# A two-layer trunk with a seven-product input projection: x read transposed, its norm applied to the results, one product of three column groups formed ahead

## The chip, the cores and the metric

The kernel runs on one core of one Trainium2 chip. The metric is the device time of one execution in microseconds (us); the time before is the median of three runs, 1564.92 us (1564.27 to 1565.75). A smaller number is better.

## The reference

Two decoder layers work on 512 tokens of width 2048, all in float32. Layer 0 is gated linear attention (GLA) with 4 heads, layer 1 latent attention (MLA) with 16 heads. Each layer normalizes its input, projects it with one wide matrix, mixes the tokens, multiplies by a SiLU gate, projects back, normalizes again and adds the residual:

```python
h = rms_norm(x, g_pre)
# layer 0
q, k, v, gate, gk_low = split(h @ w_in)        # widths 1024, 1024, 2048, 2048, 16
log_a = log_sigmoid(gk_low @ w_gk2 + b_gk) / 16
b = cumsum(log_a)                              # the decays, within chunks of tokens
o = causal(q*exp(b) @ (k*exp(-b)).T) @ v + (state carried from earlier chunks)
y = (rms_norm(o, g_onorm) * silu(gate)) @ w_out
x = x + rms_norm(y, g_post)
```

rms_norm multiplies each token's row by one number, 1/sqrt(mean of squares), and each column by a gain.

## The kernel before, in words

**Numbers of full width from fast products.** A float32 operand is kept as a rounded part hi (type fp32r) and a rest lo. One product is three matmuls of TensorE (PE): hi by hi, lo by hi, hi by lo (`mm3`, L128 to L132). ScalarE (ACT) rounds hi, VectorE (DVE) subtracts to get lo. Weights arrive as raw tiles through the DMA queue of SyncE (SP) and are split this way on the fly; some small transfers are issued by GpSimd (POOL).

**Seven products.** The projection of layer 0 is a 2x2 block product by the Strassen-Winograd scheme, which needs seven block products instead of eight. Tokens are halved (256 and 256), so are the rows of the weights (even and odd blocks of 128), and a column pair of 2 x 512 columns makes one group. There are six groups: q and k of heads 0 and 1, v and gate of head 0, of head 1, q and k of heads 2 and 3, v and gate of head 2, of head 3. `first_four` (L253) forms four of the seven products for all six groups: 8 pairs of weight rows a group, and for each pair a left and a right tile of 512 KB, three sums on DVE (L262 to L264), hi and lo of four weight blocks (L267 to L270) and 24 matmuls of 128x512. Its results are combined (u, vw) and parked in HBM (`stage`). `last_three` (L286) then takes the groups again, with 18 matmuls a pair, reads the parked results back (`done`) and combines them into c, which an evacuation function of the group takes further.

**The left side.** `start` (L320) reads x by rows, sums its squares on ACT, multiplies by the norm and the gain on DVE, transposes on PE (`xn_t`) and keeps the result h, transposed, in `ht` and, split, in the four slots of `act_hi` and `act_lo`. `left_sums` (L362) makes the sums of h that the first four products need, `left_rest` (L374) those of the last three, after all first products, since they take the same slots. `gk_low` (L499) makes the 16 columns of the decay gate by 16 plain float32 matmuls (`gkl_acc`).

**Around the groups.** `decays` (L535) makes the decays of two heads: matmuls `z`, exponentials on ACT, scans of 512 elements on DVE. `qk_evac` (L579) transposes c on PE (`qk_t`) and multiplies it by the decays. `scores` and `values` are the attention of one head. `values` writes y of a head to HBM, and `gla_rows` (L674) reads all four back, transposes them (`y_t`) and fills `act_hi` and `act_lo` for `out_proj`. That one makes four column blocks of 512, the last as two of 256. MLA follows; its first projection (`cq`) is done as two blocks of 256 columns.

**What sets the order.** The program is written in the order above, and a scheduler orders each engine's instructions at build time by its own estimate; on the chip each engine works its list strictly in order and waits by semaphores. Tiles come from pools with a fixed number of buffers. The pools of the second half of the projection (`wb`, `psb`) are opened where those of the first (`wa`, `psa`) were closed, so that a new tile waits for the old tile that lay in the same place.

Of the kernel before, what the change touches and what calls it, by code (L numbers as in the profile page):

```python
# [14 lines left out]
F32 = DT.float32  # L15
FR = DT.float32r
# [29 lines left out]
NMAC = 6  # L46
GQ0, GK0, GV0, GG0, GL0 = 0, 1024, 2048, 4096, 6144
# [3 lines left out]
R_BGK, R_GON, R_GQA, R_GKV, R_PRE = 0, 8, 12, 16, 20  # L51
NROWS = 36
# [23 lines left out]
class Trunk:  # L76
# [121 lines left out]
    def build(self):  # L198
        tc, a = self.tc, self.a
        from contextlib import ExitStack  # L200
        with ExitStack() as ctx:
# [18 lines left out]
            self.gla_rows()  # L220
# [18 lines left out]
    def raw_pair(self, w, c0, kp, rows=2, name="raw"):  # L239

        t = self.wp.tile([P, rows, 512], F32, tag=f"{name}{rows}", name=name, bufs=3)
        src = w[(2 * kp + 2 - rows) * P:(2 * kp + 2) * P, c0:c0 + 512]
        self.nc.sync.dma_start(t, src.rearrange("(k p) n -> p k n", p=P))
        return t

    def prods(self, ps, kp, slots, hi, lo, ws):
        for q, (slot, wi) in enumerate(zip(slots, ws)):
            for r in range(2):
                self.mm3(ps[2 * q + r], self.act_slot(self.act_hi, kp, slot, r),
                         self.act_slot(self.act_lo, kp, slot, r), hi[:, wi, :], lo[:, wi, :],  # L250
                         kp == 0, kp == KT // 2 - 1)

    def first_four(self, w, m, n1, n2):  # L253


        nc, v = self.nc, self.nc.vector
        ps = [self.ps.tile([P, 512], F32, tag="a", name=f"pa{q}", bufs=8) for q in range(8)]
        for kp in range(KT // 2):
            r1 = self.raw_pair(w, n1, kp, name="left")
            r2 = self.raw_pair(w, n2, kp, name="right")  # L260
            t = self.wp.tile([P, 3, 512], F32, tag="sums", name="sums", bufs=2)
            v.tensor_tensor(t[:, 0, :], r1[:, 0, :], r2[:, 0, :], ALU.add)  # L262
            v.tensor_tensor(t[:, 1, :], t[:, 0, :], r2[:, 1, :], ALU.add)
            v.tensor_tensor(t[:, 2, :], t[:, 1, :], r1[:, 1, :], ALU.add)  # L264
            hi = self.wp.tile([P, 4, 512], FR, tag="w_hi", name="w_hi", bufs=2)
            lo = self.wp.tile([P, 4, 512], FR, tag="w_lo", name="w_lo", bufs=2)
            nc.scalar.copy(hi[:, 0, :], r1[:, 0, :])  # L267
            v.tensor_tensor(lo[:, 0, :], r1[:, 0, :], hi[:, 0, :].bitcast(F32), ALU.subtract)
            nc.scalar.copy(hi[:, 1:4, :], t)  # L269
            v.tensor_tensor(lo[:, 1:4, :], t, hi[:, 1:4, :].bitcast(F32), ALU.subtract)  # L270
            self.prods(ps, kp, (0, 2, 1, 3), hi, lo, (0, 2, 1, 3))
        for r in range(2):
            p1 = self.stg([P, 512], "p1")
            nc.scalar.copy(p1, ps[r])  # L274
            nc.gpsimd.dma_start(self.stage[m, :, 0, r, :], p1)
            u = self.stg([P, 512], "u2")
            v.tensor_tensor(u, p1, ps[2 + r], ALU.subtract)
            for i, p in ((1, ps[4 + r]), (2, ps[6 + r])):
                t = self.stg([P, 512], "vw")
                v.tensor_tensor(t, u, p, ALU.add)  # L280
                nc.gpsimd.dma_start(self.stage[m, :, i, r, :], t)

# [3 lines left out]
    def last_three(self, w, m, n1, n2, evac):  # L286
# [4 lines left out]
        done = self.sp.tile([P, 3, 2, 512], F32, tag="done", name="done", bufs=1)  # L291
        nc.gpsimd.dma_start(done, self.stage[m])
        for kp in range(KT // 2):
            r1 = self.raw_pair(w, n1, kp, 1, name="left")
            r2 = self.raw_pair(w, n2, kp, name="right")
            t = self.wp.tile([P, 512], F32, tag="sum", name="sum", bufs=2)
            v.tensor_tensor(t, r2[:, 0, :], r2[:, 1, :], ALU.add)
            hi = self.wp.tile([P, 3, 512], FR, tag="w_hi", name="w_hi", bufs=2)
            lo = self.wp.tile([P, 3, 512], FR, tag="w_lo", name="w_lo", bufs=2)
            for i, x in enumerate((r1[:, 0, :], r2[:, 1, :], t)):  # L300
                nc.scalar.copy(hi[:, i, :], x)
                v.tensor_tensor(lo[:, i, :], x, hi[:, i, :].bitcast(F32), ALU.subtract)  # L302
            self.prods(ps, kp, (2, 0, 1), hi, lo, (0, 1, 2))
        for r in range(2):
            p2, q3, p7 = ps[r], ps[2 + r], ps[4 + r]
            c = [self.stg([P, 512], f"c{i}") for i in range(4)]
            v.tensor_tensor(c[0], p2, done[:, 0, r, :], ALU.add)
            evac(r, 0, c[0])
            v.tensor_tensor(c[1], q3, done[:, 1, r, :], ALU.subtract)
            evac(r, 1, c[1])  # L310
            v.tensor_tensor(c[2], p7, done[:, 2, r, :], ALU.add)
            evac(2 + r, 0, c[2])
            v.scalar_tensor_tensor(c[3], p7, -1.0, done[:, 1, r, :], ALU.mult, ALU.subtract)
            evac(2 + r, 1, c[3])
# [5 lines left out]
    def start(self):  # L320

# [8 lines left out]
        with tc.tile_pool(name="start", bufs=1, reuse_waits="tile") as xp:  # L330
# [11 lines left out]
            for s in range(ST):  # L342
                parts = self.st.tile([P, 4], F32, tag="parts", name="parts", bufs=2)
                for g in range(4):
                    self.sumsq(xt[s][:, g * 512:(g + 1) * 512], parts[:, g:g + 1])
# [714 lines left out]
```

## Time and profile before

| | us |
|---|---|
| median of three runs | 1564.92 |
| the profiled execution | 1565.73 |
| its span, first to last instruction | 1564.0 |
| PE busy in it | 1463.3 (94%) |
| DVE busy in it | 978.1 (63%) |
| ACT busy in it | 729.7 (47%) |

The profiled execution took 1.7 us more than its span and 0.8 us more than the median. PE is busy nearly everywhere, so the time is PE's list plus what PE waits, plus what it loses where its granted clock (PEclk) is below 1.00. In the tables of stages, a column gives an engine's busy time in the stage and behind it, as x, the number of its instructions; behind the engines stand the mean granted clock, the busy share of the DMA engines and their GB/s. In a timeline a row's second number is how long its instructions took from first to last.

### The profile page before, as it was taken

To read this page: it belongs to the slowest core of one execution; us is meant where nothing else is said; L and a number is where in the kernel's file an instruction comes from. 1 tells how busy PE (TensorE), PEld (TensorE's weight loads), DVE (VectorE), ACT (ScalarE), POOL (GpSimd) and SP (SyncE) were. 2 spreads that over 40 slices of the span, in tenths; PEclk is the share of its full clock that TensorE was granted. 3 is DMA by queue.
4 is the path that set the end of the run, shared out by engine and by line. 5 is a ranking of instruction groups with operands and counts; after the bars stand their busy time and mean duration, and the time that the engine had idled before them with its cause. 6 is when DMAs were issued, how large, how long until landed. Compare 5 with 4: busy or idle time off the path is not lost.

```text
span 1564.0 us, 19919 instructions
## 1 busy us (share of the span) xinstructions
PE 1463.3 (94%) x7409; PEld 1234.4 (79%) x7409; DVE 978.1 (63%) x1652; ACT 729.7 (47%) x1391; POOL 68.6 (4%) x130
## 2 busy tenths in 40 slices
PE   2699999978699799699999999999999999999998
PEld 2287887857588678588899988888888889888888
DVE  6488888879888878544347434344367777863324
ACT  6233343335366446534336424444466666753221
POOL 0200000001000000200001100000000000000000
PEclk7799999999899989799999999999999999999999
DMA  7167777745366555744326223333322221235222
GB/s 283 29 181 223 229 226 226 223 166 188 121 199 192 167 168 163 256 132 126 111 88 227 71 81 105 98 95 94 82 72 70 60 60 51 69 124 171 94 95 108
DMA packets 132961, 216.09 MB, mean 138 GB/s; under 512 B 19628, under 2 KB 56720, under 8 KB 130048
## 3 DMA queue, kind: packets, MB, share of 16 engines
q1 hardware_dynamic: 124064, 178.81, 37.4%
q0 software_dynamic: 8512, 34.89, 6.5%
q8 instruction: 58, 0.95, 0.3%
q10 hardware_dynamic: 288, 1.11, 0.2%
q14 instruction: 39, 0.32, 0.1%
HBM read 192.53 MB, written 22.25 MB: 137 GB/s over the span
## 4 chain that ended last, share of the span: by engine, by line
PE 70%; issue 18%; DVE 6%; DMA 3%; ACT 2%; POOL 1%; SPq 0%; DVEq 0%; POOLq 0%; ACTq 0%
PE yo_acc L130 8%; PE yo_acc L132 8%; PE yo_acc L131 8%; PE pb L130 4%; PE pb L131 4%; PE pb L132 3%; PE acc L132 3%; PE acc L131 3%; PE acc L130 3%; PE q_acc L132 1%; PE q_acc L131 1%; PE q_acc L130 1%; PE pt L1012 1%; DMA right<-in_l_gla_w_in_dram 1%; PE cq_acc L131 1%
## 5 line engine op out<-in xcount | busy, mean ns | idle before, releaser
L131 PE MATMUL yo_acc<-w_hi,act_lo 128*128 128x512 f32 (+1 forms) x440 | 154.1, 351 | 0.0
L132 PE MATMUL yo_acc<-w_lo,act_hi 128*128 128x512 f32 (+1 forms) x440 | 153.0, 349 | 0.0
L130 PE MATMUL yo_acc<-w_hi,act_hi 128*128 128x512 f32 (+1 forms) x440 | 152.8, 349 | 0.0
L130 PE MATMUL pa<-w_hi,act_hi 128*128 128x512 f32 x384 | 150.4, 392 | 1.4 <-ACT p L274 1.4
L131 PE MATMUL pa<-w_hi,act_lo 128*128 128x512 f32 x384 | 149.5, 389 | 0.0
L124 DVE SCALAR_TENSOR_TENSOR w_lo<-w_raw,gcol,w_hi 128x512 fp32r<-128x512 f32 (+1 forms) x98 | 64.6, 698 | 106.6 <-ACT w_hi L123 106.5
L130 PE MATMUL pb<-w_hi,act_hi 128*128 128x512 f32 x288 | 116.4, 408 | 12.7 <-ACT act_hi L384 7.6
L132 PE MATMUL pa<-w_lo,act_hi 128*128 128x512 f32 x384 | 118.3, 389 | 0.0
L123 ACT ACTIVATE w_hi<-w_raw,gcol 128x512 fp32r<-128x512 f32 (+1 forms) x98 | 61.5, 676 | 114.0 <-PE acc L132 83.9
L131 PE MATMUL pb<-w_hi,act_lo 128*128 128x512 f32 x288 | 114.0, 397 | 0.0
L132 PE MATMUL pb<-w_lo,act_hi 128*128 128x512 f32 x288 | 101.0, 398 | 0.8 <-DVE w_lo L302 0.8
L130 PE MATMUL acc<-act_hi,w_hi 128*128 128x512 f32 x256 | 99.7, 389 | 0.0
L131 PE MATMUL acc<-act_hi,w_lo 128*128 128x512 f32 x256 | 99.6, 389 | 0.0
L132 PE MATMUL acc<-act_lo,w_hi 128*128 128x512 f32 x256 | 99.1, 389 | 0.0
L270 DVE TENSOR_TENSOR w_lo<-sums,w_hi 128x1536 fp32r<-128x1536 f32 x48 | 84.2, 1754 | 15.1 <-ACT w_hi L269 15.1
L130 PEld LDWEIGHTS yo_acc<-w_hi,act_hi 128*128 128x128 f32 x440 | 83.7, 190 | 10.5 <-ACT act_hi L179 0.2
L131 PEld LDWEIGHTS yo_acc<-w_hi,act_lo 128*128 128x128 f32 x440 | 83.7, 190 | 10.0
L132 PEld LDWEIGHTS yo_acc<-w_lo,act_hi 128*128 128x128 f32 x440 | 83.6, 190 | 10.0
L116 DVE TENSOR_TENSOR w_lo<-w_raw,w_hi 128x1024 fp32r<-128x1024 f32 x32 | 39.2, 1224 | 80.9 <-ACT w_hi L115 80.8
L130 PEld LDWEIGHTS pa<-w_hi,act_hi 128*128 128x128 f32 x384 | 72.0, 188 | 20.5 <-ACT p L274 3.2
L124 DVE SCALAR_TENSOR_TENSOR w_lo<-w_raw,gon,w_hi 128x512 fp32r<-128x512 f32 (+1 forms) x80 | 47.7, 641 | 59.6 <-ACT w_hi L123 59.3
L132 PEld LDWEIGHTS pa<-w_lo,act_hi 128*128 128x128 f32 x384 | 72.1, 188 | 15.0
(331 smaller groups left out, 3636.9 us busy)
## 6 DMA issues: line engine op xcount, KB each, us to landing
right<-in_l_gla_w_in_dram SPq DMA_DIRECT2D x96, 512.0 KB, 4.3
left<-in_l_gla_w_in_dram SPq DMA_DIRECT2D x48, 512.0 KB, 4.7
w_raw<-in_l_mla_w_in_dram SPq DMA_DIRECT2D x47, 512.0 KB, 3.7
w_raw<-in_l_gla_w_out_dram SPq DMA_DIRECT2D x32, 512.0 KB, 4.0
w_raw<-in_l_mla_w_out_dram SPq DMA_DIRECT2D x32, 512.0 KB, 3.6
left<-in_l_gla_w_in_dram SPq DMA_DIRECT2D x48, 256.0 KB, 3.6
done<-stage POOLq DMA_DIRECT2D x6, 1536.0 KB, 7.4
pw_raw<-in_l_mla_w_kvb_dram SPq DMA_DIRECT2D x64, 128.0 KB, 2.6
```

The source lines that it names most:

```text
L116: nc.vector.tensor_tensor(lo, raw, hi.bitcast(F32), ALU.subtract)
L123: nc.scalar.activation(hi[:, kk, :], raw[:, kk, :], AF.Copy, scale=g)
L124: nc.vector.scalar_tensor_tensor(lo[:, kk, :], raw[:, kk, :], g, hi[:, kk, :].bitcast(F32), ALU.mult, ALU.subtract)
L130: t.matmul(out, lh, rh, start=start, stop=False)
L131: t.matmul(out, ll, rh, start=False, stop=False)
L132: t.matmul(out, lh, rl, start=False, stop=stop)
L270: v.tensor_tensor(lo[:, 1:4, :], t, hi[:, 1:4, :].bitcast(F32), ALU.subtract)
L1012: te.transpose(pt[:, o:o + P], probs[i][:, j * P:(j + 1) * P], self.ident)
```

## The change

- **x comes transposed.** Besides x by rows, the kernel gets x transposed (`xt`) and all gains as columns (`gains`), laid out before the launch. `start` loads rows of `xt` straight into `ht`. Only the gain is multiplied in. The norm is a number per token, so it commutes with the projection: `x_norm` reads x by rows through POOL in 16 tiles of 256 KB, sums the squares on ACT and keeps 1/sqrt in `rcol`, and the evacuations multiply by it (`c<-c,rcol`, `v_hi`, `gate`); the decay gate gets it through a small product (`gkl_r`).
- **One product early.** `first_one` forms the first of the seven products for groups 1 to 3 while the rest of x is still being prepared; it needs only the even rows and the first half of the tokens. `first_four` then has three products left for these groups (18 matmuls a pair of weight rows) and four for groups 4 to 6.
- **Sums in place.** The weight sums are written over the raw tiles; hi and lo of two blocks are made by one instruction each. The sums of the left side are written over `ht` (`left_swap`) well ahead, and `left_rest` only splits them, between the pairs of group 6.
- **Decays ahead.** `decays(0)` stands behind group 2 of the first products. `decays(1)` stands right behind the scores of heads 0 and 1, which are now both made before the first of the two v and gate groups.
- **Reading back.** `last_three` reads the parked results in six tiles of 256 KB with four buffers, each when it is due, instead of one tile of 1.5 MB. y of heads 0 to 2 is read back and transposed inside the last group, y of head 3 never leaves the chip (`y_rows`).
- **Full widths.** The last block of `out_proj` and the first of MLA are now 512 columns wide, over two halves of the rows.

On PE, at the start of the program, before (`xn_t` are transposes of x, `gkl_acc` the decay gate, `pa` the products of group 1):

```order
L353 MATMUL xn_t<-cf,x_89 128x128 x16
L353 MATMUL xn_t<-cf,x_97 128x128 x16
L353 MATMUL xn_t<-cf,x_99 128x128 x16
L353 MATMUL xn_t<-cf,x_101 128x128 x16
L411 MATMUL gcols<-cf,rows 128x36
L504 MATMUL gkl_acc<-ht,gkl_raw 16x512 x16
L130 MATMUL pa_388<-w_hi,act_hi 128x512
```

and of the change, from its sixteenth instruction (`p_0_89`, `p_1_90`: the first product of group 1, `p_0_192` that of group 2):

```order
L132 MATMUL p_1_90<-w_hi,act_lo 128x512
L589 MATMUL gkl_acc<-ht,gkl_raw 16x512
L133 MATMUL p_0_89<-w_lo,act_hi 128x512
...
L133 MATMUL p_1_90<-w_lo,act_hi 128x512
L589 MATMUL gkl_acc<-ht,gkl_raw 16x512 x15
L131 MATMUL p_0_89<-w_hi,act_hi 128x512
...
L131 MATMUL p_0_192<-w_hi,act_hi 128x512
```

The transposes are gone, products stand first, and 15 of the 16 gate matmuls, which read all of `ht`, stand ahead of the last quarter of the first early product.

On DVE, the decays of heads 0 and 1 before (`c` are results of the first group of the last products, `eq` and `ek` the decays, `qk_t` the transposed q and k):

```order
L307 TENSOR_TENSOR c_2815<-pb_2520,done 128x512
L309 TENSOR_TENSOR c_2816<-pb_2522,done 128x512
L554 TENSOR_TENSOR ek<-eq,ek 128x2048
L556 SCALAR_TENSOR_TENSOR eq<-restart,ek 128x512 x4
L563 TENSOR_TENSOR rest<-eq 128x12
L573 TENSOR_TENSOR ek<-eq 128x2048
...
L588 SCALAR_TENSOR_TENSOR eq<-qk_t,eq 128x4x128 x2
```

and of the change, in group 2 of the first products:

```order
L642 TENSOR_TENSOR ek<-eq,ek 128x2048
L302 TENSOR_TENSOR w_lo<-left,w_hi 128x512
L294 TENSOR_TENSOR right<-left,right 128x512
L297 TENSOR_TENSOR left<-right,left 128x512
L253 TENSOR_TENSOR w_lo<-right,w_hi 128x1024
L644 SCALAR_TENSOR_TENSOR eq<-restart,ek 128x512 x4
L295 TENSOR_TENSOR right<-right 128x512
L302 TENSOR_TENSOR w_lo<-left,w_hi 128x512
...
L661 TENSOR_TENSOR ek<-eq 128x2048
```

The same instructions have moved from the end of a group, where `qk_t` needs them, to between the weight splits of an earlier group.

On DVE, at the change from the first to the last products, of the change (`raw` is a weight tile of the last products, `ht` the sums of the left side):

```order
L253 TENSOR_TENSOR w_lo<-left,w_hi 128x1024
L315 TENSOR_TENSOR u_2483<-p_2477,pa_2159 128x512
L315 TENSOR_TENSOR u_2485<-p_2480,pa_2160 128x512
L319 TENSOR_TENSOR vw<-u_2483,pa_2161 128x512
L319 TENSOR_TENSOR vw<-u_2485,pa_2162 128x512
L464 TENSOR_TENSOR act_lo<-ht,act_hi 128x2x768
L319 TENSOR_TENSOR vw<-u_2483,pa_2163 128x512
L319 TENSOR_TENSOR vw<-u_2485,pa_2164 128x512
L349 TENSOR_TENSOR raw<-raw 128x512 x2
L253 TENSOR_TENSOR w_lo<-raw,w_hi 128x1536 x2
```

Before, twenty sums and splits of `left_rest` stood there, with the first weight splits of the last products among them. Now one split of the left side is left, and the first sums of weights stand behind all results of group 6. The first `raw` tile lies where `ht` lay, so its load is issued after that last split of `ht`.

The diff, cut to its core:

```diff
+    def split_w(self, t):
+        hi = self.wp.tile(shape, FR, tag="w_hi", name="w_hi", bufs=self.w_bufs)
+        lo = self.wp.tile(shape, FR, tag="w_lo", name="w_lo", bufs=self.w_bufs)
+        nc.scalar.copy(hi, t)
+        nc.vector.tensor_tensor(lo, t, hi.bitcast(F32), ALU.subtract)
+    def prod(self, ps, kp, slot, wt, i):
+        for r in range(2):
+            self.mm3(ps[r], self.act_slot(self.act_hi, kp, slot, r),
...
+    def first_one(self, w, n1, rows=None):
+        ps = [self.bank("a", f"p1_{r}") for r in range(2)]
...
+            wt = self.split_w(t)
+            for i in range(2):
+                self.prod(ps, 2 * g + i, 0, wt, i)
+        return ps
...
+            v.tensor_tensor(right[:, 0, :], left[:, 0, :], right[:, 0, :], ALU.add)
+            v.tensor_tensor(right[:, 1, :], right[:, 0, :], right[:, 1, :], ALU.add)
+            wr = self.split_w(right)
+            v.tensor_tensor(left[:, 1, :], right[:, 1, :], left[:, 1, :], ALU.add)
+            if have:
...
+            self.prod(ps[0:2], kp, 2, wr, 1)
+            self.prod(ps[2:4], kp, 1, wr, 0)
+            self.prod(ps[4:6], kp, 3, wl, 1)
...
-        done = self.sp.tile([P, 3, 2, 512], F32, tag="done", name="done", bufs=1)
-        nc.gpsimd.dma_start(done, self.stage[m])
...
+        def done(i, r):
+            t = self.sp.tile([P, 512], F32, tag="done", name="done", bufs=4)
+            nc.gpsimd.dma_start(t, self.stage[m, :, i, r, :])
...
+    def x_norm(self):
...
+                t = self.tmp([P, 512], F32, "x")
+                nc.gpsimd.dma_start(t, self.a["x"][0, s * P:(s + 1) * P, g * 512:(g + 1) * 512])
+                self.sumsq(t, parts[:, s, g:g + 1])
...
+    def left_swap(self, g):
+        v.tensor_tensor(h(0, 1), h(0, 0), h(0, 1), ALU.subtract)
+        v.tensor_tensor(h(0, 0), h(1, 0), h(1, 1), ALU.subtract)
+        v.tensor_tensor(h(0, 0), h(0, 0), h(0, 1), ALU.subtract)
...
+                        self.first_four(w, m, n1, n2, early[m] if m < len(early) else None)
+                        if m == 0:
+                            self.x_norm()
+                            self.constants()
+                        if m == 1:
+                            self.gk_low()
+                            self.gk_spread()
+                            with tc.issue_after(self.ln_exp.ins):
+                                self.decays(0)
...
+                    at = [self.scores(h) for h in (2 * p, 2 * p + 1)]
+                    if p == 0:
+                        self.decays(1)
+                    for i, h in enumerate((2 * p, 2 * p + 1)):
+                        self.last_three(w, 3 * p + 1 + i, *vg(h), self.vg_begin(h))
+                        if h == GH - 1:
+                            for e in range(h):
+                                self.y_rows(e)
+                        self.values(h, at[i])
+                self.y_rows(GH - 1)
...
-        self.block_s(w, 1536, 256, 0, ps, hi, lo, KT, gain=gain, evac=evac(3, 1536, 256, 0))
-        self.block_s(w, 1792, 256, 256, ps, hi, lo, KT, gain=gain, evac=evac(4, 1792, 256, 256), resident=True)
+        self.block_s(w, 1536, 512, 0, ps, hi, lo, KT, gain=gain, ks=(0, KT // 2))
+        self.block_s(w, 1536, 512, 0, ps, hi, lo, KT, gain=gain, evac=evac(3, 1536, 512, 0), resident=True,
+                     ks=(KT // 2, KT))
```

More of the change, by code (lines that the diff above doesn't have):

```diff
@@ L244, in raw_pair @@
         return t
-    def prods(self, ps, kp, slots, hi, lo, ws):
-        for q, (slot, wi) in enumerate(zip(slots, ws)):
-            for r in range(2):
[L249 to L271, printed above, removed]
-        for r in range(2):
[L273 to L281, printed above, removed]
@@ new lines, in first_four @@
+    def first_four(self, w, m, n1, n2, p1=None):
+        nc, v = self.nc, self.nc.vector
+        have = p1 is not None
+        ps1 = None if have else [self.bank("t", f"p1_{r}") for r in range(2)]
+        ps = [self.bank("a", f"pa{q}") for q in range(6)]
+        for kp in range(KT // 2):
+            left = self.raw_pair(w, n1, kp, "left")
+            right = self.raw_pair(w, n2, kp, "right")
+            v.tensor_tensor(right[:, 0, :], left[:, 0, :], right[:, 0, :], ALU.add)
[3 more added lines that the diff above has]
+            if have:
+                hi = self.wp.tile([P, 2, 512], FR, tag="w_hi", name="w_hi", bufs=self.w_bufs)
+                lo = self.wp.tile([P, 2, 512], FR, tag="w_lo", name="w_lo", bufs=self.w_bufs)
+                nc.scalar.copy(hi[:, 1, :], left[:, 1, :])
+                v.tensor_tensor(lo[:, 1, :], left[:, 1, :], hi[:, 1, :].bitcast(F32), ALU.subtract)
+                wl = hi, lo
+            else:
+                wl = self.split_w(left)
+                self.prod(ps1, kp, 0, wl, 0)
+            self.prod(ps[0:2], kp, 2, wr, 1)
+            self.prod(ps[2:4], kp, 1, wr, 0)
+            self.prod(ps[4:6], kp, 3, wl, 1)
+        if not have:
+            p1 = self.p1_out(m, ps1)
+        u = []
+        for r in range(2):
+            u.append(self.stg([P, 512], "u2"))
+            v.tensor_tensor(u[r], p1[r], ps[r], ALU.subtract)
+        for i in (1, 2):
+            for r in range(2):
+                t = self.stg([P, 512], "vw")
+                v.tensor_tensor(t, u[r], ps[2 * i + r], ALU.add)
+                nc.gpsimd.dma_start(self.stage[m, :, i, r, :], t)
@@ L304, in last_three @@
-        for r in range(2):
[L305 to L314, printed above, removed]
+            t = self.wp.tile([P, 3, 512], F32, tag="raw", name="raw", bufs=3)
@@ new lines, in last_three @@
+            self.prod(ps[0:2], kp, 2, wt, 0)
+            self.prod(ps[2:4], kp, 0, wt, 2)
+            self.prod(ps[4:6], kp, 1, wt, 1)
+        def done(i, r):
+            t = self.sp.tile([P, 512], F32, tag="done", name="done", bufs=4)
+            nc.gpsimd.dma_start(t, self.stage[m, :, i, r, :])
+            return t
+        c = lambda: self.stg([P, 512], "c")
+        d = [done(0, r) for r in range(2)]
+        for r in range(2):
+            t = c()
+            v.tensor_tensor(t, ps[r], d[r], ALU.add)
+            evac(r, 0, t)
@@ L317, in tmp0 @@
+        d = [done(1, r) for r in range(2)]
+        for r in range(2):
+            t = c()
+            v.tensor_tensor(t, ps[2 + r], d[r], ALU.subtract)
+            evac(r, 1, t)
+        for r in range(2):
+            p7 = ps[4 + r]
+            t = c()
+            v.tensor_tensor(t, p7, done(2, r), ALU.add)
+            evac(2 + r, 0, t)
+            t = c()
+            v.scalar_tensor_tensor(t, p7, -1.0, d[r], ALU.mult, ALU.subtract)
+            evac(2 + r, 1, t)
     def tmp0(self, shape, dtype, name):
@@ L581, in qk_evac @@
         nc, v = self.nc, self.nc.vector
+        nc.scalar.activation(c, c, AF.Copy, scale=self.rcol[:, t:t + 1])
         pt = self.pt("qk_t")
```

315 lines of the change are left out of this document (172 added, 143 removed).

## The prediction

> **What bounds the kernel now.** The page comes first: the span, the engines' sums and PE's granted clock in 40 slices of 39.1 us.
>
> ```profile
> span 1564.0 us, 19919 instructions
> PE 1463.3 (94%) x7409; PEld 1234.4 (79%) x7409; DVE 978.1 (63%) x1652; ACT 729.7 (47%) x1391; POOL 68.6 (4%) x130
> PEclk7799999999899989799999999999999999999999
> ```
>
> PE is the bound, but not everywhere: the clock falls in the slices where PE waits. So I cut the first 661 us where PE's load changes and read the table of stages.
>
> ```profile
> core 0: us, PE busy (x) PEld busy (x) DVE busy (x) ACT busy (x) POOL busy (x), PEclk, DMA share, GB/s
> 0.00:12.00 12.00, 0.00 (x0) 0.00 (x0) 0.21 (x2) 4.54 (x11) 0.30 (x5) 1.00 0.81 297
> 12.00:57.00 45.00, 14.85 (x66) 13.26 (x67) 41.21 (x75) 29.54 (x71) 6.39 (x11) 0.63 0.55 187
> 57.00:72.70 15.70, 15.70 (x33) 3.13 (x31) 2.10 (x10) 2.98 (x3) 1.64 (x3) 0.88 0.04 14
> 72.70:205.00 132.30, 131.58 (x578) 107.81 (x578) 106.71 (x128) 49.26 (x52) 7.54 (x14) 1.00 0.68 205
> 205.00:337.30 132.30, 131.60 (x577) 107.16 (x575) 108.91 (x135) 51.79 (x56) 10.23 (x19) 1.00 0.68 209
> 337.30:358.00 20.70, 9.00 (x20) 6.01 (x21) 16.52 (x26) 5.89 (x9) 2.15 (x4) 0.67 0.41 140
> 387.00:420.00 33.00, 19.54 (x84) 15.03 (x84) 28.43 (x45) 13.62 (x16) 0.55 (x1) 0.79 0.28 96
> 535.00:556.00 21.00, 9.12 (x40) 7.12 (x39) 17.01 (x26) 5.47 (x4) 0.54 (x1) 0.67 0.12 37
> 630.90:661.00 30.10, 17.56 (x49) 12.24 (x48) 19.55 (x32) 18.64 (x42) 6.15 (x11) 0.67 0.64 232
> ```
>
> Five places lose time: the start up to 72.7, the handover from first to last products (337.3), the decays (387 and 535), and the end of GLA (630.9). Groups 1 to 3 and 4 to 6 of the first products take 132.3 each with PE full. The list of waits names what ended PE's idle time.
>
> ```profile
> PE xn_t L353 <- DVE x L350: 27.4, 4, 13.0
> PE qk_t L584 <- DVE eq L588: 23.2, 4, 11.0
> PE pb L130 <- ACT act_hi L384: 7.6, 1, 7.6
> ```
>
> The profiled execution took 1565.73, 1.7 over its span and 0.8 over the median; I sum against it.
>
> **The start and groups 1 to 3.** PE's pace comes from a timeline of PE: 512 columns warm, 256 columns warm, 512 at the low clock.
>
> ```profile
> 333.05 0.39 PE L130 MATMUL pa<-w_hi,act_hi 128*128 128x512 f32 x1
> 333.28 0.39 PE L131 MATMUL pa<-w_hi,act_lo 128*128 128x512 f32 x1
> ...
> 799.95 0.28 PE L132 MATMUL yo_acc<-w_lo,act_hi 128*128 128x256 f32 x1
> 800.07 0.28 PE L130 MATMUL yo_acc<-w_hi,act_hi 128*128 128x256 f32 x1
> ...
> 343.94 0.63 PE L132 MATMUL pb<-w_lo,act_hi 128*128 128x512 f32 x1
> 344.37 0.63 PE L130 MATMUL pb<-w_hi,act_hi 128*128 128x512 f32 x1
> ```
>
> Starts lie 0.227, 0.12 and 0.43 apart. Before, nothing of the products was done by 72.7. Now a quarter of groups 1 to 3 (3 x 8 pairs x 6 matmuls = 144) stands in the start, and 432 matmuls of 0.227 = 98 remain. What DVE then has to do, by its timeline and groups:
>
> ```profile
> 48.10 1.28 DVE L367 TENSOR_TENSOR lsum<-ht 128x512 f32<-128x512 f32 x2
> ...
> 53.37 0.55 DVE L400 CAST cm<-masks 128x256 uint8<-128x256 int32 x1
> ...
> 58.46 0.29 DVE L436 SCALAR_TENSOR_TENSOR sin_cos<-sin_cos 128x128 f32<-128x128 f32 x1
> ```
>
> ```profile
> L116 DVE TENSOR_TENSOR w_lo<-w_raw,w_hi 128x1024 fp32r<-128x1024 f32 x32 | 39.2, 1224 | 80.9 <-ACT w_hi L115 80.8
> L551 DVE TENSOR_SCALAR eq<-z,gcol 128x512 f32<-128x512 f32 x8 | 5.9, 742 | 0.0
> L554 DVE TENSOR_TENSOR ek<-eq,ek 128x2048 f32<-128x2048 f32 x2 | 4.6, 2281 | 0.0
> L556 DVE TENSOR_TENSOR_SCAN eq<-restart,ek 128x512 f32<-128x512 f32 x8 | 9.1, 1204 | 0.1
> L573 DVE TENSOR_TENSOR ek<-eq 128x2048 f32<-128x2048 f32 x2 | 4.6, 2283 | 0.0
> ```
>
> Two adds behind each other take 1.28, so one is 0.60 to 0.64; I take 0.60, and 1.14 for a split of 1024, since the group's mean of 1.22 includes what overlaps its neighbour. A pair of weight rows costs three sums, one split of 1024 and one of 512: 3 x 0.60 + 1.14 + 0.60 = 3.54, times 24 = 85. The results of three groups add 18 x 0.60 = 10.8, the trigonometry 5.5 (53.4 to 58.9), the gate's gk an estimated 2.6. The moved decays(0): 4 x 0.742 + 2.28 + 4 x 1.204 + 2.28 = 12.3, with its small copies 13. Sum 117, over PE's 98: DVE becomes the bound of these groups. It can start on them when the early splits are over. For these, 4.2 MB of `xt`, twelve left and three right tiles (7.9 MB) come through SP, and 4.2 MB of x through POOL: 16.3 MB. The rate:
>
> ```profile
> 16.00:24.00 8.00, 2.70 (x13) 2.30 (x13) 6.12 (x12) 7.86 (x25) 0.00 (x0) 0.75 1.06 400
> ```
>
> At 400 GB/s that is 41 us, at the 297 of the first 12 us it is 55. The early tiles also turn slowly: from the fourth on, a buffer comes free only after a cast, a split and six matmuls, and each of the following rounds is a load of 4.7 and about 2.3 of cast and split. I take 54, near the upper end. On POOL's list the last five tiles of x stand behind the writing of group 1's early product, and on DVE's the norm (`rcol`) stands ahead of the first sum of `right`; as the early product itself needs no norm, both end with the early splits. The third group's last product then ends at 54 + 117 + 2 = 173 instead of 205.0: **32 gained**. If PE alone bounds, it starts at 12 and needs 144 x 0.227 = 33 for the early products, 14 for the gate matmuls and 98: 157, 48 gained. The 16 gate matmuls, about 14 of the 15.7 us of PE's work between 57.0 and 72.7, move ahead of products; DVE's work covers them, and without that cover they would cost those 14. The gate's transfers, of 32 KB, now stand in POOL's list between the parked results of group 1, for which nobody waits before the last products. The transposes `xn_t` and their waits go.
>
> Groups 4 to 6 keep four products: DVE's 109 of 132.3 lies under PE's. **0.**
>
> **Handover.** Before, 20.7 us held 20 matmuls, 4.5 of work: 16.2 lost. Now one split of the left side stands behind PE's last product, and the load of the first raw tile behind that split, as its buffer lies where `ht` lay. Its load:
>
> ```profile
> 342.30 6.32 DMA right<-in_l_gla_w_in_dram
> ...
> left<-in_l_gla_w_in_dram SPq DMA_DIRECT2D x48, 512.0 KB, 4.7
> ```
>
> Split 1.7, load 4.7 to 6.3, sum 0.6, ACT's cast 1.5 (near the 1.48 of the row below), low clock for about 3 us 1.6: about 10.6. **6 gained** (4 to 8).
>
> ```profile
> L269 ACT CAST w_hi<-sums 128x1536 fp32r<-128x1536 f32 x48 | 71.0, 1479 | 22.8 <-DVE sums L264 22.8
> ```
>
> **Decays.** Between 387 and 420 PE idles for 13.5 us, mostly in the waits for `eq`, and after its pauses it runs for some us at half pace, two times 1.6 to 1.8: 17. With the decays done two groups earlier, only norm, transposes and product stand behind c, an estimated 3. **14 gained.** 535 to 556: 11.9 idle and 2 for the clock, 14. Here decays(1) moves into the following v and gate group, where DVE has about 33 + 13 = 46 us of work to PE's 18 x 8 x 0.227 = 33 and some 7 of scores and values: some 6 are lost there. **8 gained** (4 to 11). DVE's own idle time in the group before cannot take them, since they stand behind the scores on its list.
>
> **End of GLA.** Before, the chain waits for y to come back:
>
> ```profile
> 646.19 9.76 DMA y<-yd
> ```
>
> The transposes come in fours, by the timeline of PE:
>
> ```profile
> 663.22 0.60 PE L683 MATMUL y_t<-cf,y 128*128 128x128 f32 x4
> ```
>
> 30.1 us pass, with 17.56 of PE's work in them at clock 0.67, and of the 64 transposes 52 still follow, (0.60 - 0.27) / 3 = 0.11 apart: 5.7. So 35.8 stand before. Now the first three heads lie in the last group and the last head needs no DMA, but DVE's list behind the last product has 8 c, 4 v_lo, 4 gate, 4 sg, 13 splits of y and 4 products by the norm: 37 at 0.6 = 22, with hops 24.5. **11 gained** (5 to 16, as 4 us of splits may overlap the products or the hops may double).
>
> **Full widths.** 768 matmuls of 256 columns in `out_proj` and 384 in MLA become 576 of 512. A pair costs 0.24, one of 512 costs 0.227: 576 x 0.013 = 7.5. **7 gained** (5 to 8).
>
> Sum: 32 + 0 + 6 + 14 + 8 + 11 + 7 = 78; 1565.7 - 78 = 1488 for a profiled execution, 1487 for the median. With the terms' ends in mind, that case's own range is 1476 to 1500.
>
> **Rivals.** *PE bounds the early groups.* If DVE's extras find room while PE does the gate matmuls and the early products, group 3 ends at 157: 16 less, 1471. For it: DVE idles at times in any stage (106.7 of 132.3). Against: its own list adds up to 117.
>
> *The parked results come late.* Six `done` tiles share four buffers; the fifth and sixth are asked for only when the first c are made.
>
> ```profile
> done<-stage POOLq DMA_DIRECT2D x6, 1536.0 KB, 7.4
> stage<-vw POOLq DMA_DIRECT2D x24, 256.0 KB, 2.8
> xo<-in_x_dram POOLq DMA_DIRECT2D x16, 256.0 KB, 8.0
> ```
>
> A transfer of this size takes 2.8 to 8.0 from POOL; four c cover 2.4. Up to 4 us may so be lost in each of six groups: 24, 1511. For it, the 8.0; against it, PE has other banks to go on with, and a single tile is asked for early. The Trainium skill, "DMA: Bandwidth & Descriptors", section "Measured (HBM→SBUF, 128 partitions, SWDGE, issued from GpSimd)", speaks against this part of the change: batch transfers to 1 MiB and more for 75% of peak. In the rows above, six of 256 KB in series are 17 to 48 against 7.4 for one of 1.5 MB, so that the trace agrees for a series; whether they come in series no run here shows.
>
> *The norm comes late; slower.* `x_norm` takes 16 tiles of 256 KB through POOL in three buffers, each freed by a sum of squares on ACT, and every result and decay needs it. If the ring goes one tile at a time, 16 x (8.0 + 0.64 + some 0.7 of issue and semaphore) = 150 us pass before the norm stands, and since DVE's list holds the norm ahead of its first sum of `right`, group 3 ends at about 150 + 117 = 267 instead of 173: 94 more, 1582. It turns slower than before where the norm comes later than 54 + 78 = 132, at over 8.2 a tile in series; three in flight take 16 x 9.3 / 3 = 50 and hide. The sum of squares:
>
> ```profile
> L190 ACT ACTIVATE junk<-x 128x512 bf16<-128x512 f32 x16 | 10.3, 643 | 7.4 <-DMA x<-in_x_dram 7.3
> ```
>
> For it, 16.3 MB compete at the start and SP's queue has the larger share; against it, three buffers. The Trainium skill, "SBUF — State Buffer", section "Who interferes with whom", says that GpSimd cannot write descriptors while DVE runs a one-source operation in its fast mode; DVE's work of the start is of two-source kind, and no run here shows a POOL transfer held back by DVE.
>
> *The early product isn't early*, because gate matmuls stand in PE's list ahead of its last quarter. Under DVE's bound this costs nothing; it lies in the first case.
>
> **Numbers.** Main case 63%: 1487, the prediction. PE bounds: 20%, 1471. Late parked results: 14%, 1511. Late norm: 3%, 1582. 1466 to 1512 holds the main case, and both near rivals but for their outer ends. 0.2% is 3.1 us, about what a measurement of this kernel can tell from no change. Only the late norm, or several terms that all fail, gives slower: 0.03; the same 0.01; faster 0.96.
>
> **What would show it.** Right: the third group's last product near 173 with DVE over 90% busy from 54 on; the handover near 11; no wait of `qk_t` over 3; decays(1) with PE idle about 6; 24 us from the last product of GLA to `yo_acc` at full pace; matmuls of 512 in all of `out_proj`. Wrong: DVE waiting for `rcol` or for weight tiles in groups 1 to 3, `c` waiting for `done`, group 3 ending before 160, or DVE work behind the last product that PE waits for longer than before.

## The result and the profile after

The changed kernel takes 1540.63 us (median of four runs, 1537.79 to 1545.33) against 1565.34 before (1564.27 to 1566.08): a ratio of 0.9846, 95% interval 0.9815 to 0.9876. It is faster, but by 25 us where 78 were forecast, and the time lies outside the range of 1466 to 1512. The profiled execution took 1537.97, span 1536.2: 27.8 less than the one before. Its page:

```profile
span 1536.2 us, 18609 instructions
PE 1452.7 (95%) x6776; PEld 1188.2 (77%) x6776; DVE 946.4 (62%) x1498; ACT 728.5 (47%) x1261; POOL 87.2 (6%) x167
PEclk9999999989999999899999999999999999999999
```

The hole at the start is gone from the row of PE's clock, and the dip at the handover is small. PE's share has hardly risen, though: something takes a little everywhere. The table of stages is cut at the events that the prediction names:

```profile
core 0: us, PE busy (x) PEld busy (x) DVE busy (x) ACT busy (x) POOL busy (x), PEclk, DMA share, GB/s
12.00:66.60 54.60, 51.20 (x176) 31.06 (x176) 38.70 (x55) 41.44 (x76) 10.63 (x20) 1.00 0.87 303
66.60:191.40 124.80, 109.33 (x445) 83.10 (x445) 111.64 (x173) 56.65 (x68) 11.90 (x23) 0.96 0.72 220
191.40:331.70 140.30, 134.32 (x577) 106.99 (x576) 115.70 (x141) 56.48 (x56) 9.70 (x18) 1.00 0.65 196
331.70:340.30 8.60, 0.00 (x0) 0.00 (x0) 4.11 (x5) 1.59 (x2) 5.27 (x10) 0.68 0.83 265
421.60:475.00 53.40, 47.12 (x191) 36.84 (x190) 46.82 (x61) 35.84 (x51) 5.39 (x10) 0.94 0.55 168
610.60:643.00 32.40, 20.68 (x88) 14.42 (x86) 22.77 (x38) 21.59 (x47) 7.42 (x14) 0.79 0.35 116
```

The rows are the start up to the first left product of group 1 (66.6), groups 1 to 3 (their last product ends at 191.4), groups 4 to 6, the handover, the group with decays(1), and the end of GLA from the first c of its last group. Against the prediction's terms, in us of the two profiled executions:

| term | forecast gain | measured |
|---|---|---|
| start and groups 1 to 3 (205.0 to 173 / 191.4) | 32 | 13.6 |
| groups 4 to 6 (132.3 / 140.3) | 0 | -8.0 |
| handover, to the 20th matmul of the last products (20.7 / 15.5) | 6 | 5.2 |
| decays(0): from the first c of the first group to that of the second (56.7 / 45.0) | 14 | 11.7 |
| decays(1): the two groups that lost and gained them (44.5 and 56.2 / 53.4 and 47.8) | 8 | -0.5 |
| the other two groups of the last products (40.1 and 44.0 / 41.9 and 45.9) | 0 | -3.7 |
| end of GLA with the y_t that followed (34.5 / 32.4) | 11 | 2.1 |
| full widths, from the output projection on (900.5 without y_t / 893.2) | 7 | 7.3 |

These add up to 27.7 of the 27.8. The border between the first two rows is the end of group 3's last product. By the first results of group 3 (203.2 before, 194.1 now), which the runs below are compared by, the two rows are 9.1 and -3.5. Three terms hold: the handover, decays(0) and the widths. Four fail, and these are the ones in which DVE's list was costed by its sum of work. The two other groups of the last products had no term in the sum and lost 3.7. The waits show where DVE stands:

```profile
DVE raw L349 <- DMA raw<-in_l_gla_w_in_dram: 50.5, 36, 3.8
...
DVE right L294 <- DMA left<-in_l_gla_w_in_dram: 33.6, 26, 3.1
...
PE pb L131 <- ACT w_hi L252: 15.6, 4, 8.7
...
PE y_t L782 <- DVE act_lo L181: 10.0, 6, 3.0
...
PE qk_t L673 <- DVE ek L679: 3.8, 4, 2.2
```

The wait of `qk_t` for the decays has fallen from 23.2 to 3.8, as forecast. The row of `left` is new: in the first products DVE waits 26 times for a weight tile. The row of `raw` is the same wait in the last products, where the sum is made in place too; before, DVE waited there 10 times for `right`, 11.2 us in all. What these 50.5 us cost was not tested. The chain of waits in group 5 shows what the wait for `left` does:

```profile
262.84 1.23 DVE w_lo L253
...
264.08 3.75 DMA left<-in_l_gla_w_in_dram
...
267.93 0.06 DVE right L294
...
268.54 1.23 DVE w_lo L253
...
269.78 3.66 DMA left<-in_l_gla_w_in_dram
...
273.54 0.06 DVE right L294
...
274.15 1.23 DVE w_lo L253
...
275.39 4.99 DMA left<-in_l_gla_w_in_dram
...
280.47 0.06 DVE right L294
...
281.08 1.23 DVE w_lo L253
```

It is a closed loop. A split of `left` ends, its tile may be loaded anew, the load takes 3.7 to 5.0, the sum of that new tile runs, and only behind it in DVE's list stands the next split. One turn takes 5.6 to 6.9; PE needs only 24 x 0.227 = 5.45 for the four products of a pair.

### The profile page after: what moved, and what is told of

Its sections match the earlier page's. It is cut to its first block, busy times and chain, and to the rows that moved or that the text cites. A ratio compares the mean times of both kernels' runs of the same rounds, so it can differ in the third digit from the quotient of the medians.

```text
span 1536.2 us, 18609 instructions
## 1 busy us (share of the span) xinstructions
PE 1452.7 (95%) x6776; PEld 1188.2 (77%) x6776; DVE 946.4 (62%) x1498; ACT 728.5 (47%) x1261; POOL 87.2 (6%) x167
## 4 chain that ended last, share of the span: by engine, by line
PE 74%; DVE 10%; DMA 9%; ACT 4%; issue 3%; SPq 0%; DVEq 0%; POOL 0%; ACTq 0%; POOLq 0%
PE yo_acc L131 7%; PE yo_acc L133 7%; PE yo_acc L132 7%; DMA left<-in_l_gla_w_in_dram 6%; PE acc L133 4%; PE acc L131 4%; PE acc L132 4%; PE pb L131 3%; PE pb L132 3%; PE pb L133 3%; DVE w_lo L253 2%; PE pa L131 2%; PE pa L132 2%; DMA raw<-in_l_gla_w_in_dram 2%; PE pa L133 2%
## 5 line engine op out<-in xcount | busy, mean ns | idle before, releaser
L131 PE MATMUL yo_acc<-w_hi,act_hi 128*128 128x512 f32 x352 | 137.1, 390 | 1.3 <-ACT w_hi L124 1.3
L132 PE MATMUL yo_acc<-w_hi,act_lo 128*128 128x512 f32 x352 | 136.9, 389 | 0.0
L133 PE MATMUL yo_acc<-w_lo,act_hi 128*128 128x512 f32 x352 | 136.1, 389 | 0.0
L125 DVE SCALAR_TENSOR_TENSOR w_lo<-w_raw,gcol,w_hi 128x512 fp32r<-128x512 f32 x89 | 63.3, 747 | 101.8 <-ACT w_hi L124 101.7
L124 ACT ACTIVATE w_hi<-w_raw,gcol 128x512 fp32r<-128x512 f32 x89 | 59.8, 716 | 111.1 <-PE acc L133 83.9
L133 PE MATMUL pa<-w_lo,act_hi 128*128 128x512 f32 x288 | 95.3, 397 | 5.9 <-DVE w_lo L302 4.3
L252 ACT CAST w_hi<-raw 128x1536 fp32r<-128x1536 f32 x48 | 70.8, 1478 | 58.8 <-PE pb L132 43.6
L125 DVE SCALAR_TENSOR_TENSOR w_lo<-w_raw,gon,w_hi 128x512 fp32r<-128x512 f32 x64 | 45.1, 748 | 84.0 <-ACT w_hi L124 84.0
L252 ACT CAST w_hi<-right 128x1024 fp32r<-128x1024 f32 x48 | 50.5, 1051 | 93.4 <-DVE right L295 39.2
L253 DVE TENSOR_TENSOR w_lo<-raw,w_hi 128x1536 fp32r<-128x1536 f32 x48 | 83.9, 1750 | 10.7 <-ACT w_hi L252 8.9
L131 PEld LDWEIGHTS pb<-w_hi,act_hi 128*128 128x128 f32 x288 | 56.0, 195 | 35.2 <-ACT w_hi L252 17.3
```

Source lines behind the costliest of these rows:

```text
L124: nc.scalar.activation(hi[:, kk, :], raw[:, kk, :], AF.Copy, scale=g)
L125: nc.vector.scalar_tensor_tensor(lo[:, kk, :], raw[:, kk, :], g, hi[:, kk, :].bitcast(F32), ALU.mult, ALU.subtract)
L131: t.matmul(out, lh, rh, start=start, stop=False)
L132: t.matmul(out, ll, rh, start=False, stop=False)
L133: t.matmul(out, lh, rl, start=False, stop=stop)
L252: nc.scalar.copy(hi, t)
```

## The experiments

The theory after the result was that sums in place tie DVE to the loads, that decays and reading back are dear because DVE's list is dense where they stand, and that the start is held by PE or by weights. Rivals stand with each run. Across runs that do not share a chip, the ratio to the kernel before, measured on the same chip, is compared.

**e0_after**, the change once more. 

> The changed kernel once more, as the measure for the others of this chip: 1538 to 1545, its third group's last product near 191, group 6 near 332, the output projection from 643.


Measured: 1539.99 (1537.33 to 1542.44), ratio 0.9838 (0.982 to 0.9857).

**e1_ring**

```diff
-            t = self.wp.tile([P, 2, 512], F32, tag="left", name="left", bufs=3)
+            t = self.wp.tile([P, 2, 512], F32, tag="left", name="left", bufs=4)
...
-self.w_bufs = 4
+self.w_bufs = 3
```

> Four buffers instead of three for the raw weight tiles of the first products, three instead of four for their hi and lo, the same memory. Theory 'the ring of loads': a tile whose sums are made in place is held until its split is over, so the next load is asked for late and DVE waits 34 us for left tiles; then these waits fall to under 10 and the time by 8 to 14. Rival 'DVE's own work': its list is full from 80 to 160 anyway, and the waits lie where PE is the bound; then the time falls by 0 to 3. A second rival, that three buffers of hi and lo are too few: slower by up to 5.


Measured: 1549.43 (ratio 0.9901, 0.9885 to 0.9917), slower by 9. The first left product came at 61.4 instead of 66.6 and the first results of group 3 at 185.3 instead of 194.1, but from there to the end of group 6 it took 150.5 instead of 137.6: PE waited for the `w_lo` of the left tile there, 10.2 us against 5.5. The run has two edits in one, and neither theory can be read from it; the direction is that of the second rival, too few buffers of hi and lo.

**e2_gate1, e7_x1, e8_gate1x1**: what holds the start. e2 leaves out 15 of the 16 gate matmuls, e7 15 of the 16 loads of x by rows, e8 both.

```diff
-        for k in range(KT):
-            nc.tensor.matmul(ps[0:GRANK, :], raw[:, k, :], self.ht[:, k, :], ...)
+        nc.tensor.matmul(ps[0:GRANK, :], raw[:, 0, :], self.ht[:, 0, :], ...)
...
+                if s == g == 0:
                     nc.gpsimd.dma_start(t, self.a["x"][...])
```

> Leaves out 15 of the 16 matmuls of the decay gate (only the first 128 rows are summed). Theory 'PE is full in the start': PE works from 12 to 66 without a gap on 144 early products (33) and the gate matmuls (14); without them the early products end near 54 and the whole is 9 to 13 shorter. Rival 'the early splits and loads set the start': they end near 62 in any case, 0 to 3 shorter.

> Leaves out 15 of the 16 loads of x by rows (the sums of squares are all taken from the first tile, with the same work on ACT). Theory 'the bytes of the start': 18.8 MB come in by 64 at about 300 GB/s, 3.9 MB less make the first of the three left products begin at 54 to 58 instead of 66.7, and the whole is 7 to 12 shorter. Rival 'the turns of the weight buffers set it': it begins at 63 or later, 0 to 3 shorter.

> Leaves out both the 15 gate matmuls and the 15 loads of x by rows. Theory 'two walls at one place': PE's list in the start (12 + 33 + 14 and some waits = 62) and the arrival of the weights (62 to 66) each hide the other, as leaving out one alone moved the first left product only from 66.7 to 66.3 and to 63.3; without both it begins at 54 to 58. Rival 'a third thing, the turns of the buffers of left and of hi and lo, holds both': 62 or later.


Measured: 1535.79 (ratio 0.9804, 0.9782 to 0.9825), 1546.01 (0.9876, 0.9857 to 0.9895) and 1540.95 (0.984, 0.9825 to 0.9854). The timeline of PE has the first left product of group 1 at, in this order:

```profile
66.25 0.39 PE L131 MATMUL pa<-w_hi,act_hi 128*128 128x512 f32 x1
```

```profile
63.25 0.39 PE L131 MATMUL pa<-w_hi,act_hi 128*128 128x512 f32 x1
```

```profile
63.19 0.39 PE L131 MATMUL pa<-w_hi,act_hi 128*128 128x512 f32 x1
```

Both theories fall, and their combination too: neither the gate's 14 us of PE nor 3.9 MB of loads set this point. The whole of e2 is some 5 shorter than e0, between its two forecasts, and the two intervals overlap. ACT is busy 41.4 of 54.6 there and the four-buffer runs (above and below) begin at 61 to 62, so a turn of buffers and ACT's casts are likely, but that is not shown. The chain of the change agrees with it: a sum of squares on ACT waits for x until 55.3, the cast of an early left tile comes behind it at 56.6, its split ends at 58.8, and the load into the tile so freed lands at 63.9, where the first sum of `right` waits for it. Without x, in e7 and e8, that sum runs at 59.5, and the next cast on ACT waits until 61.5 for an early product on PE.

**e3_dec1, e9_nodec1**: decays(1) one group later, and left out.

```diff
-                    if p == 0:
-                        self.decays(1)
                     for i, h in enumerate((2 * p, 2 * p + 1)):
+                        if h == 1:
+                            self.decays(1)
```

> The decays of heads 2 and 3 are written one group later, behind the values of head 0. Theory 'two loads on DVE in one group': scores, values and decays together make DVE's list the bound of the group from 421 to 475 (47 of 54 busy); it falls to about 44, the next group grows from 42 to 45 at most, so 5 to 8 shorter. Rival 'the loss moves along': the next group grows by the same 9, 0 to 2 either way.

> Leaves out the decays of heads 2 and 3 (the tiles of heads 0 and 1 are used again). Theory 'they are dear wherever they stand': the group from 421.6 to 475 falls from 53.4 to 43 to 45, and the whole is 8 to 11 shorter. Rival 'that group is long for the scores and values of heads 0 and 1': it stays at 48 or more, 0 to 5 shorter.


Measured: 1536.9 (ratio 0.982, 0.9805 to 0.9835) and 1528.61 (0.9764, 0.9748 to 0.9781). The stages of the second and the third of the last groups, moved:

```profile
421.20:466.20 45.00, 43.66 (x191) 35.42 (x190) 37.08 (x46) 30.16 (x47) 5.39 (x10) 1.00 0.66 202
466.20:517.50 51.30, 43.22 (x175) 33.38 (x174) 42.25 (x56) 30.66 (x44) 6.80 (x12) 0.93 0.54 173
```

and left out:

```profile
419.90:463.30 43.40, 42.05 (x183) 33.99 (x182) 34.56 (x43) 24.79 (x40) 5.39 (x10) 1.00 0.67 207
463.30:507.60 44.30, 41.01 (x177) 32.64 (x176) 32.59 (x41) 26.48 (x41) 6.75 (x12) 1.00 0.62 202
```

Moved, the loss moves along: 53.4 becomes 45.0 and 41.9 becomes 51.3, so the rival was right there. Left out, the first of the groups falls to 43.4 and the whole by 11.6, by the ratios; 2.3 of this stand ahead of the first c, where there are no decays(1). Over the two groups together the decays cost 7.6 in the first place (95.3 against 87.7) and 8.6 in the second (96.3), although DVE is busy only 47 of 53 and 42 of 51 there.

**e4_nodec0, e5_nodec0_ring, e13_ring5, e10_sep**: DVE's load in groups 1 to 3, number of tiles, and sums of their own.

```diff
-                                self.decays(0)
...
+                    if p == 0:
+                        self.decays(0)
                     self.last_three(w, 3 * p, *qk(p), self.qk_evac)
```

All four runs have this edit. Besides, e5 has `left` and `right` with 4 buffers, e13 with 5, and e10, with 3 buffers, has the sums in a tile of their own and `left` split by two instructions, one for the raw row and one for the sum:

```diff
+            t = self.wp.tile([P, 3, 512], F32, tag="sums", name="sums", bufs=2)
-            v.tensor_tensor(right[:, 0, :], left[:, 0, :], right[:, 0, :], ALU.add)
+            v.tensor_tensor(t[:, 0, :], left[:, 0, :], right[:, 0, :], ALU.add)
...
```

> The decays of heads 0 and 1 go back from the first products to the first group of the last products, where they stand among the weight splits ahead of c. Theory 'DVE's list is the bound of the first three groups': 13 us of DVE work leave group 2, its end comes 8 to 13 earlier than 151; in the group of the last products DVE has 22 + 13 of 36 us, so it pays back 3 to 10 there, 0 to 8 shorter in all. Rival 'loads, not work, set the first three groups': group 2 and 3 end within 3 of before, and the whole is up to 10 longer.

> As the run before, and the memory that the decays leave free gives four buffers to the raw tiles of the first products with all four of hi and lo. Theory 'the ring of loads costs in groups 1 to 6': against the run before, group 6 ends 8 to 14 earlier, the waits of DVE for left tiles halve. Rival 'the transfers themselves are the limit' (308 GB/s in the start): the ring only changes when bytes are asked for, group 6 ends within 4 of the run before.

> As the run with the decays of heads 0 and 1 in the last products, and the three weight sums go to a tile of their own with two buffers, as in the kernel before, so that right is free after two sums and left after its own. Theory 'the sums in place cost in groups 4 to 6': against that run these groups fall from 138 to 132 or 134, as before. Rival 'it is the six banks and the evacuation in DVE's list': 137 to 140.

> As the run with decays(0) in the last products, sums in place, with five buffers for the raw tiles and four for hi and lo: as many pairs under way as with a tile of their own for the sums. Theory 'too few tiles under way': group 6 ends near 302 and the time is near 1519. Rival 'a tile is given back too late, at the pace of PE, whatever their number': group 6 ends at 315 or later, 1525 or more.


Measured: 1535.02 (ratio 0.9809, 0.9784 to 0.9834), 1527.2 (0.976, 0.9743 to 0.9777), 1518.62 (0.970, 0.9669 to 0.973) and 1532.05 (0.9788, 0.9773 to 0.9803). In e4 the first results of group 3 come at 183.7 instead of 194.1, of which 2.5 are there in group 1 already, ahead of the decays. About 5 us are left at the end, by medians; the intervals overlap. DVE's work did hold those groups. DVE's waits for the left tiles, in e4, with five tiles, and with sums of their own:

```profile
DVE right L294 <- DMA left<-in_l_gla_w_in_dram: 32.8, 29, 2.7
```

```profile
DVE right L294 <- DMA left<-in_l_gla_w_in_dram: 31.6, 27, 3.0
```

```profile
DVE sums L295 <- DMA left<-in_l_gla_w_in_dram: 1.8, 2, 1.2
```

Five tiles wait as much as three. Four buffers (e5) do shorten the whole, 1535.0 to 1527.2, but only 3.0 of this is there at the end of group 6. Group 6 ends at 321.9 (e4), 318.9 (four), 318.0 (five), and at 302.0 with sums of their own; from the first results of group 3 to there it takes 138.2 in e4 and 132.2 in e10. So the sums in place cost 20 us by the end of group 6, 14 of them in groups 1 to 3, and the number of tiles does not cure it. The rival of e5, that the transfers are the limit, falls with this too: e10 loads the same weights. DVE's list at the end of group 6 shows why, the last first sum and the splits of `left` that still stand behind it, in the change:

```profile
314.70 0.69 DVE L294 TENSOR_TENSOR right<-left,right 128x512 f32<-128x512 f32 x1 [0.94 <-DMA left<-in_l_gla_w_in_dram]
316.98 1.22 DVE L253 TENSOR_TENSOR w_lo<-left,w_hi 128x1024 fp32r<-128x1024 f32 x1
...
320.45 1.22 DVE L253 TENSOR_TENSOR w_lo<-left,w_hi 128x1024 fp32r<-128x1024 f32 x1
...
324.39 1.22 DVE L253 TENSOR_TENSOR w_lo<-left,w_hi 128x1024 fp32r<-128x1024 f32 x1
```

and in e10:

```profile
284.57 0.69 DVE L295 TENSOR_TENSOR sums<-left,right 128x512 f32<-128x512 f32 x1
...
287.01 0.68 DVE L310 TENSOR_TENSOR w_lo<-left,w_hi 128x512 fp32r<-128x512 f32 x1
...
293.77 0.68 DVE L310 TENSOR_TENSOR w_lo<-left,w_hi 128x512 fp32r<-128x512 f32 x1
```

The list of the change runs its first sums ahead by all three tiles that there are, so that each needs the tile that the split just ahead of it has freed; with five tiles four such splits are left behind the last sum, and the wait is the same. In e10 two are left of three tiles, and a load has time to land. There, too, `left` comes free by its split. Whether the two buffers of the sums or the earlier split of the raw row sets this order, e10 doesn't separate. The stages of e10:

```profile
66.00:167.00 101.00, 96.93 (x426) 78.24 (x425) 98.64 (x153) 47.02 (x60) 12.03 (x23) 1.00 0.91 282
167.00:302.00 135.00, 134.72 (x595) 111.09 (x593) 118.56 (x165) 58.37 (x79) 10.22 (x19) 1.00 0.64 196
```

In the first row DVE is busy 98.6 of 101 and PE 96.9, and in groups 4 to 6 PE is full again. (The border at 167.0 is early: group 3's last product ends at 170.9, so groups 1 to 3 take 105 and groups 4 to 6 take 131.) The Trainium skill, "Perfetto Trace Analysis", section "Optimization Strategy", reads gaps that repeat on the engine that should be full as a possible sign of too little SBUF for the next tile, by count or size of buffers. With 5.6 to 6.9 a turn the gaps repeat here, and memory for two more tiles each of `left` and `right` changed the wait from 32.8 to 31.6: the measurement decides against the count.

**e6_end, e11_endb**: the end.

```diff
-                        if h == GH - 1:
-                            for e in range(h):
-                                self.y_rows(e)
                         self.values(h, at[i])
+                        if h == GH - 1:
+                            for e in range(h):
+                                self.y_rows(e)
```

and for e11 also `tag="b", bufs=6` for the tile `y_t` instead of the two banks (PSUM buffers) `pt`.

> The reading back of heads 0 to 2 is written behind the values of head 3, not ahead. Theory 'PE's own list in series with DVE's': at the end 48 transposes that wait for splits stand in PE's list ahead of the 9 us of products of head 3; with these first, the stretch from the first c of the last group to the output projection falls from 32 to about 25. Rival 'DVE's count of operations is the bound': as many splits remain and three move behind the last product, 31 to 34.

> As the run with the reading back behind the values of head 3, and its transposes go to the six banks that the last products have left, not to two. Theory 'the ring of two banks': there one block of transposes cost 1.26, PE, ACT and DVE taking turns, while DVE needs 0.6 to 0.7; the stretch from the first c of the last group to the output projection falls from 38.5 to 28 to 31, and the whole from 1546 to about 1537. Rival 'ACT and DVE in turn, whatever the banks': 36 or more.


Measured: 1545.87 (0.9883, 0.9863 to 0.9903) and 1535.28 (0.9803, 0.9789 to 0.9818). From the first c to the output projection it takes 38.5 and 28.8, against 32.4. The first theory, that PE's list is in the wrong order, falls: with head 3 first it is slower. In e6 DVE's timeline shows the pace of the transposes:

```profile
635.31 0.69 DVE L181 TENSOR_TENSOR act_lo<-y_t,act_hi 128x512 fp32r<-128x512 f32 x1 [0.76 <-ACT act_hi L180]
636.38 0.69 DVE L181 TENSOR_TENSOR act_lo<-y_t,act_hi 128x512 fp32r<-128x512 f32 x1 [0.38 <-ACT act_hi L180]
637.83 0.69 DVE L181 TENSOR_TENSOR act_lo<-y_t,act_hi 128x512 fp32r<-128x512 f32 x1 [0.76 <-ACT act_hi L180]
```

Two blocks take 2.52, one bank waiting for the other: 1.26 a block. In e11:

```profile
625.76 1.28 DVE L181 TENSOR_TENSOR act_lo<-y_t,act_hi 128x512 fp32r<-128x512 f32 x2
...
627.56 1.88 DVE L181 TENSOR_TENSOR act_lo<-y_t,act_hi 128x512 fp32r<-128x512 f32 x3
```

Three take 1.88: with six banks DVE runs without a break. In the order of e6 the ring of two banks was the limit. No run has six banks in the order of the change, so what they are worth there is not shown.

**e14_noearly, e15_noearly_sep**: the early product left out, of the change and of e10.

```diff
-        p1 = [self.first_one(w, self.order[0][0], even)]
+        p1 = []
+        for k in range(0, KT, 2):
+            even(k)
```

> The changed kernel without the product formed early: groups 1 to 3 form four products each, everything else is as in the change. Theory 'with sums in place the early product buys little, as groups 1 to 3 are held by DVE and its loads': 1540 to 1550, group 3 ends at 190 to 200. Rival 'it is what carries the gain of the start': a quarter of three groups, 33 us of PE, comes back, 1555 or more.

> The same taken out of the run with the sums in a tile of their own and decays(0) in the last products (1518.6). Theory 'there it is worth its matmuls': PE is full in groups 1 to 3, so 15 to 30 longer, 1534 to 1548. Rival 'the start is held by the weights in any case': 1517 to 1526.


Measured: 1546.4 (0.9872, 0.9848 to 0.9895) and 1526.02 (0.9753, 0.9734 to 0.9771): the early product is worth 5 to 6 in the change, where the intervals overlap, and 7 to 8 with sums of their own. The first expectation holds in time (though group 3's results come at 204.3), in the second the theory falls and the rival's upper end is met. In e15 the first results of group 3 come at 182.0 instead of 169.8, and 203.2 before: without the early product, 21 of 33 remain, so most of the gain there is of the rest of the new start.

**e16_best**: e10 with the end of e11.

> What the runs point to together: sums in a tile of their own, decays(0) in the last products, the reading back behind the values of head 3 with its transposes in six banks. If the pieces add up: 1518.6 less about 4, 1512 to 1517. Rival 'the end is paced by DVE there too': 1518 to 1521.


Measured: 1513.89 (1513.1 to 1516.3), ratio 0.9672 (0.9657 to 0.9688): better than both kernels, by 51 and by 26, and within the forecast of the pieces added up. Its step of 4 to 5 us beyond e10 lies within the intervals.

## Why the prediction was wrong

- **Direction and the pieces with one stage** were right: faster, the handover (10.6 lost forecast; 15.5 less 4.5 of work = 11.0 measured), decays(0) (14, measured 11.7), the widths (7, measured 7.3). The pace of 0.227 held. The 11.7 of decays(0) is no net gain, though: in e4, where these decays stand in the last products again, the way from the end of group 6 to the second group's first c grows by 6.4 only, and group 3 comes 10 earlier.
- **The start and groups 1 to 3** (32, measured 13.6). Two steps fail. "I take 54" for the end of the early splits was 66.6: the bytes were 18.8 MB rather than 16.3 (0 to 64, by 234 GB/s in the first 12 us and 308 behind), yet leaving out 3.9 MB moved it to 63.3 only; what holds it stays open. And "117" of DVE work became 125 us: DVE was busy 111.6 in them, less than the sum said, and waited 11.6 for left tiles, for which the sum had nothing. That DVE, not PE, is the bound was right (e4: 13 us less of it, 10 earlier); that it is never kept waiting was not.
- **Groups 4 to 6: "DVE's 109 of 132.3 lies under PE's. 0."** This is the step that failed most plainly: -8.0 (-3.5 by the first results). A share of busy time below 1 was taken for cover. The prediction gave the sums in place no term: who frees the buffer now, and what stands ahead of that in its list, was not asked. The runs showed a wait of 20.2 us for left tiles in these groups, and a turn of 5.6 to 6.9 where PE needs 5.45. With sums of their own the two parts together are 20 shorter at group 6 (302.0 against 321.9), and the ratio falls by 0.011, 17 us.
- **decays(1)** (8, measured -0.5). The loss in the new group was forecast as 46 - 40 = 6, from averages; against the group without them it was 9 (53.4 against 44.5, and 51.3 against 41.9 in e3). DVE's work of 46 was right (46.8); the step that failed is to set it against PE's as an average. The decays fall together with c, v_lo, gate and values in the first half of the group: from 422.8 to 445.7 DVE has no gap, and two splits of weights run there, where PE uses one each 18 x 0.227 = 4.1. The gain in the group that lost them was 8.4, not 14; why it was not more is open.
- **The end** (11, measured 2.1). In "37 at 0.6 = 22, with hops 24.5" DVE's work was right: it is busy 22.8 of the 32.4. The hops failed, 2.5 in the sum and 9.6 measured. DVE works nearly without a break from 610.6 to 628.9 = 18.3, and behind it come head 3's products, norm and transposes in series, 14 more, in which it waits for ACT's norm and casts. e11 has the end at 28.8, by order and banks together. Before, the end is 34.5 from the first c, not 35.8: the window to 661.0 held products of the output projection already.
- **The rivals.** *Parked results late* did not happen: no wait of DVE for `done` stands in the list, and PE's 2.0 and 1.5 at the first c of a group are those of the evacuation. The rule of 1 MiB from the Trainium skill, "DMA: Bandwidth & Descriptors", section "Measured (HBM→SBUF, 128 partitions, SWDGE, issued from GpSimd)", cited there, did not decide anything here: 36 of 256 KB took 3.6 in the median, ran ahead, and no engine waited for them. *Norm late* did not happen either: the norm stands at 62. *PE bounds the early groups* was not met in the change; e10 comes near to it, with PE 96.9 and DVE 98.6 of 101. The range missed because no rival put a price on a weight tile that comes back late, though the list of signs names that wait.

## What to carry to other kernels

When a buffer is reused in place, ask which instruction now frees it and what stands ahead of that instruction in its engine's list: if a transfer into the same ring must land first, load time enters each turn, and more buffers did not shorten the waits here. Work moved into a group with room on average can cost as if there were little, when it falls into the group's dense part: 13 us of decays cost 8 to 9 here. Cost it against the dense stretch, not the mean. In e6 a bank came round through PE, ACT and DVE in 2.52, so two banks gave a block each 1.26; count banks before operations.

## What was not expected of the hardware and its records

A third of the loss in groups 4 to 6 is not idle time: PE shows 134.3 busy with 577 matmuls in the change, 131.6 with 577 before and 134.7 with 595 in e10. Something stretches the busy column, probably short stalls, so matmuls in a stage say more than its share. Leaving out work made the kernel slower once (e7, 15 loads fewer, ratio 0.9876 against 0.9838 of e0): the lists on all engines are ordered anew by the scheduler with each edit, and group 2 took 48.6 there instead of 46.3. Differences of some 5 us between such kernels may come from that alone, which no run here tests; those of e2, e4 and e14 are of this size.
